# A grouped softmax: five tiles for six, one multiply a row, attached waits, loops not aligned

## Chip, cores and metric

The kernel runs on one core of one Trainium2 chip. The metric is the device time of one execution in microseconds (us); before the change it was 1332.67 us, the median of three runs (1332.51 to 1333.12). A run on the chip also leaves a profile; its one-page summary is called the page below, and its records of single instructions and transfers the trace. All profiled runs fell in the fast state, clock 1.000.

## The reference

An fp32 array of 16384 rows of 4352 numbers; each row is cut into eight groups of 544, and each group goes through a softmax.

```python
x_g = x.reshape(B, N, 8, 544)            # B, N = 4, 4096
x_g = x_g - x_g.max(axis=-1, keepdims=True)
exp = np.exp(x_g)
out = exp / exp.sum(axis=-1, keepdims=True)
```

285 MB come in and 285 MB go out.

## The kernel before

A tile is 256 rows of the array: 128 partitions with two rows each, 4352 KB. There are 64 tiles. The tiles live in a ring of six buffers. Three engines run their own programs. SyncE, called the queue's program below, issues the loads and stores. VectorE takes a row's eight maxima, later the reciprocals of the sums, and multiplies. ScalarE makes the exponentials and sums.

```python
def take(engine, sem, n=1):                    # a wait as an instruction of its own
    engine.sem_inc(sem, -n).wait_op(sem, n, "sem-ge")

def vector_scale(s):
    take(nc.vector, exp_done)
    nc.vector.reciprocal(out=rs[:, s, :], in_=sm[:, s, :]).then_inc(rec_done, 1)
    take(nc.vector, rec_done)
    xr = row(s)
    for g in range(G):
        i = nc.vector.tensor_scalar_mul(
            out=xr[:, g, :], in0=xr[:, g, :], scalar1=rs[:, s, g:g + 1])
    i.then_inc(scaled, 1)

def step(t, source, target):                   # the queue's program
    store(t, target)                           # waits until tile t is scaled
    take(nc.sync, stored[(t - 1) % NT], 16)    # the tile before has left
    load(t + AHEAD, source)                    # AHEAD = NT - 1
# ... cut ...
nc.sync.sem_inc(stored[NT - 1], 16)
for t in range(AHEAD):
    load(t, xt[t])
with nc.Fori(0, ring_turns, engines=OrderedEngineSet([nc.sync.engine]),
             head_slot={nc.sync.engine: 0}) as u:
    for t in range(NT):
        step(t, turn_in[u, t], turn_out[u, t])
# ... cut ...
with nc.Fori(0, turns, engines=OrderedEngineSet([nc.scalar.engine]),
             head_slot={nc.scalar.engine: 54}):
    for s in range(S):
        scalar_exp(s)
# ... cut ...
vector_max(0)
with nc.vector.Fori(0, turns):
    for s in range(S):
        vector_max((s + 1) % S)
        vector_scale(s)
```

With `head_slot` a loop asks for a place (slot) of its first instruction in a block of program: slot 0 for the queue's loop, slot 54 for ScalarE's. Such a loop is called aligned below.

## Time and profile before

| | before |
|---|---|
| time, median | 1332.67 us |
| span of the profiled run | 1331.4 us |
| transfers busy, of 16 DMA engines | 99.4% |
| VectorE / ScalarE busy | 78% / 57% |
| step of the queue (one load, one store) | 20.65 us |

A span runs from the first to the last instruction. The kernel is bound by its transfers, and the other engines wait for them; the prediction shows the lines.

### The profile page before, as it was taken

The numbers are of one execution on the slowest core, as the hardware profiler recorded it, in microseconds if no ns is written. First come the engines' busy times: TensorE is split into PE (matmuls) and PEld (weight loads), VectorE is DVE, ScalarE is ACT, GpSimd is POOL, SyncE is SP. The second block draws the span as 40 slices with busy tenths as digits, with TensorE's granted clock in tenths as the row PEclk, the third lists the DMA queues.
The fourth block names the chain that finished last, engine by engine and source line by source line (L and its number), as shares of the span: only waits on it lengthen the run. The fifth ranks groups of instructions, "written<-read, shape, count | busy, mean of one in ns | idle before, by whom it ended". The sixth has DMA issues, their size and how long they took to land. (4 is left out here: it accounts for less than half of the span.)

```text
span 1331.4 us, 4367 instructions
## 1 busy us (share of the span) xinstructions
DVE 1041.6 (78%) x1280; ACT 764.4 (57%) x2049; POOL 0.2 (0%) x4
## 2 busy tenths in 40 slices
DVE  4999987787877878778778787787877878778771
ACT  3777765655656556555565565655655556555560
POOL 0000000000000000000000000000000000000000
DMA  9999999999999999999999999999999999999997
GB/s 400 419 434 433 433 433 433 433 428 431 432 434 433 435 434 435 433 430 430 433 433 434 433 435 435 435 430 430 432 432 435 434 432 435 435 434 430 430 431 308
DMA packets 18441, 570.51 MB, mean 429 GB/s; under 512 B 2048, under 2 KB 2048, under 8 KB 2048
## 3 DMA queue, kind: packets, MB, share of 16 engines
q1 hardware_dynamic: 18432, 570.43, 99.4%
q14 instruction: 9, 0.07, 0.0%
HBM read 285.21 MB, written 285.21 MB: 428 GB/s over the span
## 5 line engine op out<-in xcount | busy, mean ns | idle before, releaser
L81 ACT ACTIVATE xt<-xt,mx 128x544 f32<-128x544 f32 x1024 | 751.2, 734 | 532.3 <-ACTq L56 532.3
L65 DVE TENSOR_REDUCE mx<-xt 128x8 f32<-128x4352 f32 x128 | 599.1, 4681 | 236.5 <-DVEq L56 236.4
L73 DVE TENSOR_SCALAR xt<-xt,rs 128x544 f32<-128x544 f32 x1024 | 434.1, 498 | 19.2 <-DVEq L56 0.2
L81 ACT ACTIVATION_READ_ACCUMULATOR xt<-xt,mx 128x1 f32 x1024 | 191.0, 187 | 0.0
L69 DVE RECIPROCAL rs<-sm 128x8 f32<-128x8 f32 x128 | 24.6, 192 | 4.2 <-DVEq L56 4.2
L120 ACT ACT_TABLE_LOAD x1 | 1.3, 1283 | 0.9 <-SPq L49 0.9
L153 POOL MEMSET const-bfloat16-1.0<- 128x1 bf16 x1 | 0.1, 103 | 0.0
L153 POOL MEMSET const-uint8-127<- 128x1 uint8 x1 | 0.1, 102 | 0.0
L153 POOL MEMSET const-float32-1.0<- 128x1 f32 x1 | 0.1, 100 | 0.0
L153 POOL MEMSET const-float32-0.0<- 128x1 f32 x1 | 0.1, 99 | 0.2 <-issue 0.2
## 6 DMA issues: line engine op xcount, KB each, us to landing
xt<-in_x_dram SPq DMA_DIRECT2D x64, 4352.0 KB, 30.7
out_dram<-xt SPq DMA_DIRECT2D x64, 4352.0 KB, 40.5
```

What stands on the lines that cost most here:

```text
L65: nc.vector.reduce_max(out=mx[:, s, :], in_=row(s), axis=X, negate=True).then_inc(max_done, 1)
L69: nc.vector.reciprocal(out=rs[:, s, :], in_=sm[:, s, :]).then_inc(rec_done, 1)
L73: i = nc.vector.tensor_scalar_mul(out=xr[:, g, :], in0=xr[:, g, :], scalar1=rs[:, s, g:g + 1])
L81: i = nc.scalar.activation(out=xr[:, g, :], in_=xr[:, g, :], func=Exp, bias=mx[:, s, g:g + 1], scale=1.0, accum_out=sm[:, s, g:g + 1],)
L120: nc.scalar.preload_act_table(Exp)
L153: nc = _bacc.Bacc("TRN2", target_bir_lowering=False, num_devices=1)
```

## The change

Its intent is a plainer kernel: less memory for the ring, fewer instructions, and no aligned loops.

```diff
-    NT = 6
+    NT = 5
 ...
     def vector_scale(s):
-        take(nc.vector, exp_done)
-        nc.vector.reciprocal(out=rs[:, s, :], in_=sm[:, s, :]).then_inc(rec_done, 1)
-        take(nc.vector, rec_done)
+        nc.vector.reciprocal(out=rs[:, s, :], in_=sm[:, s, :]).wait_op(
+            exp_done, s + 1, "sem-ge").then_inc(rec_done, 1)
         xr = row(s)
-        for g in range(G):
-            i = nc.vector.tensor_scalar_mul(
-                out=xr[:, g, :], in0=xr[:, g, :], scalar1=rs[:, s, g:g + 1])
-        i.then_inc(scaled, 1)
+        nc.vector.tensor_tensor(
+            out=xr,
+            in0=xr,
+            in1=rs[:, s, :].unsqueeze(2).to_broadcast([P, G, Dg]),
+            op=mybir.AluOpType.mult,
+        ).wait_op(rec_done, s + 1, "sem-ge").then_inc(scaled, 1)
 ... (the maximum and the exponential get attached waits in the same way)
-    with nc.Fori(
-            0, ring_turns, engines=OrderedEngineSet([nc.sync.engine]),
-            head_slot={nc.sync.engine: 0}) as u:
+    with nc.sync.Fori(0, ring_turns) as u:
 ...
-    with nc.Fori(
-            0, turns, engines=OrderedEngineSet([nc.scalar.engine]),
-            head_slot={nc.scalar.engine: 54}):
+    with nc.scalar.Fori(0, turns):
         for s in range(S):
             scalar_exp(s)
+        nc.scalar.sem_inc(max_done, -S)
 ...
+        nc.vector.sem_inc(exp_done, -S)        # at the end of VectorE's turn
+        nc.vector.sem_inc(rec_done, -S)
```

## The prediction

Passages that no trace or run of this case shows are cut out of the text, each cut marked. The sum: 1332.7 plus 0 to 2 us (start) and 0 to 1 us (end), put at 1333.3. The multiply's 4.69 us is an estimate from the maximum of the same row, which took 4.68 us (4.69 in the last line of the third view), and the 2% for the first rival rests on that estimate alone. The microseconds allowed at the turns and the 3 us for a changed mix of loads and stores are guesses; no trace showed them.

> **What bounds the kernel now.** I read the page first (busy shares, then the slices), then the queue's own issues in the timeline, then VectorE's timeline in the steady middle, at the start and at the end.
>
> ```profile
> DVE 1041.6 (78%) x1280; ACT 764.4 (57%) x2049; POOL 0.2 (0%) x4
> DMA  9999999999999999999999999999999999999997
> ...
> q1 hardware_dynamic: 18432, 570.43, 99.4%
> ...
> L81 ACT ACTIVATE xt<-xt,mx 128x544 f32<-128x544 f32 x1024 | 751.2, 734 | 532.3 <-ACTq L56 532.3
> L65 DVE TENSOR_REDUCE mx<-xt 128x8 f32<-128x4352 f32 x128 | 599.1, 4681 | 236.5 <-DVEq L56 236.4
> L73 DVE TENSOR_SCALAR xt<-xt,rs 128x544 f32<-128x544 f32 x1024 | 434.1, 498 | 19.2 <-DVEq L56 0.2
> ...
> xt<-in_x_dram SPq DMA_DIRECT2D x64, 4352.0 KB, 30.7
> out_dram<-xt SPq DMA_DIRECT2D x64, 4352.0 KB, 40.5
> ```
>
> The DMA engines are busy 99.4% of the span; VectorE is busy 78% and ScalarE 57%. VectorE's idle time stands almost wholly before the maximum (236.4 us), which waits for landings. So the transfers are the bound.
>
> ```profile
> 607.77 0.34 SPq L93 DMA_DIRECT2D xt<-in_x_dram  x1
> 608.36 0.35 SPq L97 DMA_DIRECT2D out_dram<-xt  x1
> 628.43 0.34 SPq L93 DMA_DIRECT2D xt<-in_x_dram  x1
> 628.95 0.35 SPq L97 DMA_DIRECT2D out_dram<-xt  x1
> ```
>
> One load and one store go out every 20.66 us, so a tile costs the queue 20.66 us and a transfer 10.33 us (2 x 4.456 MB in 20.66 us is 431 GB/s). 128 transfers of 10.33 us are 1322 us; the other 9 us of the span are the start and the last landing. A load takes 30.7 us to land, a store 40.5 us: with 10.33 us each, these are places three and four in a queue. On average (30.7 + 40.5)/20.66 = 3.4 transfers are under way.
>
> ```profile
> 597.32 4.68 DVE L65 TENSOR_REDUCE mx<-xt 128x8 f32<-128x4352 f32 x1 [4.04 <-DVEq L56]
> 601.92 0.19 DVE L69 RECIPROCAL rs<-sm 128x8 f32<-128x8 f32 x1
> 602.27 3.39 DVE L73 TENSOR_SCALAR xt<-xt,rs 128x544 f32<-128x544 f32 x8
> 605.58 4.68 DVE L65 TENSOR_REDUCE mx<-xt 128x8 f32<-128x4352 f32 x1
> 610.17 0.19 DVE L69 RECIPROCAL rs<-sm 128x8 f32<-128x8 f32 x1
> 610.51 3.39 DVE L73 TENSOR_SCALAR xt<-xt,rs 128x544 f32<-128x544 f32 x8
> 617.98 4.69 DVE L65 TENSOR_REDUCE mx<-xt 128x8 f32<-128x4352 f32 x1 [4.08 <-DVEq L56]
> ```
>
> This is one tile on VectorE: two rows of 8.26 us (597.32 to 605.58), then 4.08 us of waiting for the next landing. That 4.08 us is its whole room. The chain of waits to the end is cut off at the last multiply, which ends at 1301.5, 30 us before the span does: the rest is stores draining.
>
> [...] The loop ends of this trace cause no visible wait on VectorE, whose loop is not aligned before either; I allow a few microseconds a turn for the other engines.
>
> **The change, part by part.**
>
> (a) One multiply a row. Eight scalar multiplies of 3.39 us together become one two-tensor multiply of 4.69 us (estimate from [...] the reduction's 4.68). A row on VectorE becomes 8.26 + 1.30 = 9.56 us, a tile 19.1 us against 20.66 for its transfers. Busy time becomes 599.1 + 24.6 + 128 x 4.69 = 1224 us, 92%. Its room shrinks from 4.1 to 1.5 us a tile but stays above zero: cost to the end in the steady part, 0.
>
> (b) Waits attached to instructions. Before, each wait is its own semaphore instruction: 320 on VectorE of 21 ns (6.7 us in all), 128 on ScalarE of 17 ns. They go, and a few count-downs once a turn come. The busy chain of a row overlaps or hides most of them. Gain on the path: 0, since VectorE isn't the bound.
>
> (c) Five tiles for six. Time around the ring before: 6 x 20.66 = 124.0 us = 30.7 (load) + 29.0 (landing at 597.32 to the end of the tile's second multiply, 20.66 + 4.68 + 0.19 + 0.15 + 3.39) + 40.5 (store) + what is left, 23.8 us, in which a finished tile waits for its store to be issued because the queue's program stands at an earlier store's completion. With five: 5 x 20.66 = 103.3 = 30.7 + (29.0 + 1.3) + 40.5 + 1.8. The idle wait falls from 23.8 to 1.8 us, with the DMA queue just as deep. So the sixth tile was slack. Even if compute ran later, the first thing to shrink would be the queue of 3.4 transfers: more than two of them (about 25 us of work) can go before the engines run dry.
>
> (d) The start. Four loads are put out rather than five, so the queue is full up to about 15.95 + 3 x 10.33 = 46.9 us (the first maximum starts at 15.95, when load 0 has landed). The first store went out at 39.13; two longer multiplies come before it, so 41.7. That is 5 us ahead of the end of the loads. The first load needed 14.9 us from issue to landing, 4.5 us over its 10.33, part of it before the first byte, so the margin is 1 to 5 us. Load 4 follows at once. Later stores come every 19.1 us, slower than before but faster than 20.66, so the lead grows. Cost: 0 to 2 us.
>
> (e) The end. When the last tile lands (1278.58 before), four stores of 10.33 us remain instead of five, and the last must be there after three of them, 31.0 us later. Its compute before: 1278.58 to 1301.49, 22.9 us, with the multiplies of three rows in it: the one of the tile before, its first row's (beside which the exponentials run) and its last. Adding 1.3 us for each at most: 26.8 us. That is 4 us early, again less some of the start-up time. Cost: 0 to 1 us.
>
> (f) Loops not aligned. Twelve turns. VectorE can win back 1.5 us a tile, 7.7 us a turn, and ScalarE, which had 532 us of idle time, much more. The queue's program has two to three transfers ahead of it. Up to a few microseconds a turn are hidden.
>
> Sum: 1332.7 + 0 (steady) + 0 to 2 (start) + 0 to 1 (end) - 0, so 1333.3.
>
> **The rivals.**
>
> First: VectorE becomes the bound. It does if the multiply takes over about 5.5 us for a row (4.69 + 1.5/2 = 5.4). For it: 92% busy, with a broadcast operand not in the trace before. [...] If the multiply took 5.8 us, a tile would take 21.4 us, and 64 of them with start and end 1370 + 25 = about 1395 us. [...] I give this 2%.
>
> Second: the ring is too short. The 1.8 us in (c) could turn negative through jitter in landings or a stall at a loop's end. Then stores go out later and loads, which wait for stores, too. If the engines ran dry for 2 us at each of 12 turns, 1357 us. Against it: what shrinks first is the depth of the queue, not its busy time. I give a visible loss, over 5 us, 5%, most of it still within 2%.
>
> Third: the change is faster, because fewer semaphore and multiply instructions let VectorE hand over stores sooner. Against it: stores already wait 23.8 us before, so nothing earlier than that helps[...]. Under 1%. A shallower or differently mixed queue could change the rate by a few tenths of a per cent either way; that is most of my range.
>
> **Range and chances.** The steady rate varies between 428 and 435 GB/s among the slices, but averages over turns repeat to 0.05% in the three runs. Start and end can cost up to 3 us, a changed mix of loads and stores some 3 us either way, a small loss at the turns 3 us more. So 1333.3, with 1330 to 1339. Faster by over 2% would need 1306 us, under the 1322 us that the transfers take: 1%. Slower by over 2% needs 1360 us, the first rival or a bad case of the second: 3%.
>
> **What would show it right or wrong.** Right: DMA stays at 99% with the same GB/s; the multiply's group has 128 instructions of about 4.69 us; VectorE is about 92% busy; its wait before the maximum falls from 236 to about 236 - 128 x 1.3 = 70 us; ScalarE's busy time is unchanged; store issues come 0.5 us after load issues or up to some microseconds later, still every 20.66 us. Wrong: slices in which DMA falls below 9 or GB/s under 425, which names the stage (first two slices: start; last two: end; all over: ring or VectorE); a multiply of over 5.5 us; VectorE without any wait for landings in the steady part. [...]

## More of the kernel before

The page's part on DMA queues has one line for the data and this one for the program itself, with packets, MB and the share of sixteen engines' time:

```profile
q14 instruction: 9, 0.07, 0.0%
```

Nine packets of program, and a share that rounds to nothing.

## The result, and the profile after

The changed kernel took 1329.93 us, the median of four runs (1328.73 to 1330.95), against 1332.79 us for four runs of the kernel before. The ratio is 0.9978 with a 95% interval of 0.9961 to 0.9995. A ratio here is the mean time of one kernel's fast runs over that of the other's of the same rounds, so it is not quite the ratio of the medians quoted. The time lies 0.07 us below the predicted range of 1330 to 1339, and the prediction's sum had only terms that cost something, while the change gained 2.9 us. A miss of 0.07 us is far inside the spread of the four runs, so landing inside the range would have been luck: the gain has no term in the sum. It is worth asking where it came from.

The page of the kernel after, in the same parts as the prediction showed of before (busy engines, DMA slices, queues, groups of instructions, issues):

```profile
DVE 1207.7 (91%) x384; ACT 764.4 (58%) x2049; POOL 0.2 (0%) x4
...
DMA  9999999999999999999999999999999999999998
...
q1 hardware_dynamic: 18432, 570.43, 99.7%
q14 instruction: 3, 0.02, 0.0%
...
L82 ACT ACTIVATE xt<-xt,mx 128x544 f32<-128x544 f32 x1024 | 751.3, 734 | 539.2 <-DVE mx L63 539.2
L63 DVE TENSOR_REDUCE mx<-xt 128x8 f32<-128x4352 f32 x128 | 599.1, 4681 | 94.8 <-DMA xt<-in_x_dram 94.8
L72 DVE TENSOR_TENSOR xt<-xt,rs 128x4352 f32<-128x4352 f32 x128 | 600.6, 4692 | 4.4
...
xt<-in_x_dram SPq DMA_DIRECT2D x64, 4352.0 KB, 30.6
out_dram<-xt SPq DMA_DIRECT2D x64, 4352.0 KB, 40.3
```

Nearly everything is as foretold. The multiply takes 4692 ns. VectorE is busy 91%, and its wait before the maximum has shrunk from 236.4 to 94.8 us. Loads and stores land after 30.6 and 40.3 us, so the queue of transfers is as deep as with six tiles. What was not foretold is the second queue line: three packets of program for nine.

The queue's timeline after, in the steady middle (start, duration, engine, line, what was issued):

```profile
616.14 0.34 SPq L96 DMA_DIRECT2D xt<-in_x_dram  x1
616.66 0.35 SPq L100 DMA_DIRECT2D out_dram<-xt  x1
636.71 0.34 SPq L96 DMA_DIRECT2D xt<-in_x_dram  x1
637.63 0.35 SPq L100 DMA_DIRECT2D out_dram<-xt  x1
```

A step is 20.57 us (616.14 to 636.71), where the prediction's lines of before have 20.66 us. And the first maximum, which waits for the first landing, begins earlier. VectorE's timeline at the start (in brackets, how long the engine stood idle and what ended it), before:

```profile
15.95 9.28 DVE L65 TENSOR_REDUCE mx<-xt 128x8 f32<-128x4352 f32 x2 [15.95 <-DVEq L56]
```

and after:

```profile
13.90 9.28 DVE L63 TENSOR_REDUCE mx<-xt 128x8 f32<-128x4352 f32 x2 [13.90 <-DMA xt<-in_x_dram]
```

So there are two gains: 2.05 us at the first landing, and a shorter step. These two profiled runs lie further apart (1333.15 and 1328.73 us, 4.4 apart) than the medians, so the sizes read from them overstate the gain of 2.9 us.

**One level deeper: the sixteen engines.** A transfer is cut into 128 packets of 34,816 bytes, eight for each of sixteen DMA engines. In the trace most packets take 1288 ns, in both kernels (from 400 to 900 us 5964 of 6221 before, 6007 of 6222 after). A landing raises its semaphore sixteen times (2048 counts for 128 transfers), read here as once for each engine, and the wait ends with the sixteenth. I read these times from the trace's records, and call "lag" the time from the middle engine's count (between the eighth and the ninth) to the last one's.

| | first landing | its lag | lag at landing 33 of 128 | lag at the last but one | step, 400 to 900 us | last landing |
|---|---|---|---|---|---|---|
| before | 15.82 | 2.10 | 5.70 | 9.47 | 20.645 | 1330.04 |
| after | 13.88 | 0.38 | 4.15 | 3.74 | 20.567 | 1325.48 |

All in us. 20.567 us is sixteen packets of 1.2854 us, which is a packet's 1.288 us less the 3 ns or so by which neighbours overlap in the trace: in the steady part after, the last engine loses nothing. Before, the last engine loses another 0.078 us with each tile, through to the end; this is called the drift below. The middle engine gains nothing from the change (1330.04 - 9.46 = 1320.6 us before, 1325.48 - 3.74 = 1321.7 after, with the lags of the very last landing). The whole gain is that the last engine lags less.

The packet records of the kernel before show four packets of program of 8 KB, at 1.9, 7.1, 7.6 and 13.3 us, while the first loads are under way; they took 0.31 to 0.41 us each, 1.3 us in all. At the first landing the last engine came 1.31 us after the second last. The kernel after has no such packet before 38.7 us. This suggests a theory: program packets share the DMA engines with the data, and one engine that has to carry them lands its share of every transfer late.

### The profile page after: what moved, and what is told of

The parts are those of the page before. It is cut to its first block, busy times and chain, and to the rows that moved or that the text cites. A ratio compares the mean times of both kernels' runs of the same rounds, so it can differ in the third digit from the quotient of the medians.

```text
span 1326.8 us, 3155 instructions
## 1 busy us (share of the span) xinstructions
DVE 1207.7 (91%) x384; ACT 764.4 (58%) x2049; POOL 0.2 (0%) x4
## 2 busy tenths in 40 slices
DMA packets 18435, 570.46 MB, mean 430 GB/s; under 512 B 2048, under 2 KB 2048, under 8 KB 2048
## 3 DMA queue, kind: packets, MB, share of 16 engines
q1 hardware_dynamic: 18432, 570.43, 99.7%
## 5 line engine op out<-in xcount | busy, mean ns | idle before, releaser
L63 DVE TENSOR_REDUCE mx<-xt 128x8 f32<-128x4352 f32 x128 | 599.1, 4681 | 94.8 <-DMA xt<-in_x_dram 94.8
L72 DVE TENSOR_TENSOR xt<-xt,rs 128x4352 f32<-128x4352 f32 x128 | 600.6, 4692 | 4.4
## 6 DMA issues: line engine op xcount, KB each, us to landing
xt<-in_x_dram SPq DMA_DIRECT2D x64, 4352.0 KB, 30.6
out_dram<-xt SPq DMA_DIRECT2D x64, 4352.0 KB, 40.3
```

The source lines that it names most:

```text
L63: i = nc.vector.reduce_max(out=mx[:, s, :], in_=row(s), axis=X, negate=True)
L72: nc.vector.tensor_tensor(out=xr, in0=xr, in1=rs[:, s, :].unsqueeze(2).to_broadcast([P, G, Dg]), op=mybir.AluOpType.mult,).wait_op(rec_don ...
```

## The experiments

The theories: A, program fetched beside the first loads makes the gain. B, the ring of five tiles does. The prediction's own view was that nothing gains. Fifteen kernels ran, all correct.

### Which part of the change

**Five tiles only.** `NT = 6` becomes `NT = 5` in the kernel before.

> The kernel before with five tiles instead of six, nothing else. Theory A (the gain is instruction fetch: fewer instruction packets beside the first loads, so that no DMA engine starts late): still eight multiplies a row, so the first landing stays at 15.5 to 16 us and the time within 0.1% of before, 1332 to 1334. Theory B (the gain is the ring: with five tiles the sixteen DMA engines are spread apart less by the end): 1329 to 1331, and the steady step 20.57 us instead of 20.65. My recorded prediction held the sixth tile to be slack: 0.

1333.23 us, ratio 1.0004 (0.9987 to 1.0020); step 20.645 us. The ring gains nothing and loses nothing: theory B falls. The first landing came at 15.19 us, a little before the expected 15.5.

**One multiply only.** The eight `tensor_scalar_mul` of the kernel before become one `tensor_tensor`, with everything else left.

> The kernel before with one two-tensor multiply a row, six tiles, aligned loops and separate waits kept. Theory A (instruction fetch): VectorE's program shrinks by seven instructions a row, so the first landing comes at 14 to 14.5 us and the time is 1329.5 to 1331.5. Theory B (the ring): 1332 to 1334. VectorE about 92% busy either way; if VectorE were close to being the bound, over 1335.

1332.86 us, ratio 1.0001 (0.9984 to 1.0018). VectorE's shorter program did not help: theory A in its first form, that the multiplies' instructions are what is fetched, falls too. The four packets were still there, at 1.9, 6.6, 8.0 and 13.7 us.

**Loops and waits only.** The changed kernel with `NT = 6` and the eight multiplies put back.

> The changed kernel with six tiles and eight multiplies a row put back: only attached waits, counts once a turn and unaligned loops are left of the change. Theory A in its second form (padding for aligned loops is what is fetched): first landing at 14 to 14.5 us, 1330 to 1331.5. If the eight multiplies are what is fetched: 1332 to 1334 and the landing stays near 15.8. Theory B: 1332 to 1334.

1329.42 us, ratio 0.9977 (0.9960 to 0.9994), first landing 13.87 us, step 20.567 us. This part alone makes the whole gain. What the packets hold, padding or other program, no trace shows.

**The changed kernel again**, on the same chip.

> The changed kernel itself, on the chip of the three runs beside it: 1328.5 to 1331 again. If on this chip it does not differ from the kernel before, the 0.2% is a matter of chip or moment, not of the change.

1329.53 us, ratio 0.9981 (0.9965 to 0.9998). The gain repeats.

**Alignment or waits?** First the kernel before with its two aligned loops left unaligned, waits as they were:

```diff
-            head_slot={nc.sync.engine: 0}) as u:
+            ) as u:
-            head_slot={nc.scalar.engine: 54}):
+            ):
```

> The kernel before with the two aligned loops left unaligned, and nothing else; waits stay separate. If the alignment is the cause [...]: first landing near 14 us, 1329 to 1330.5. If the attached waits and the counts once a turn are the cause: landing near 15.5, 1332 to 1333.5.

1329.77 us, ratio 0.9978 (0.9961 to 0.9994), step 20.568 us. VectorE's first maximum in this run:

```profile
14.21 9.28 DVE L65 TENSOR_REDUCE mx<-xt 128x8 f32<-128x4352 f32 x2 [14.21 <-DVEq L56]
```

Then the reverse: the changed kernel with the two `head_slot` options put on.

> The changed kernel with the two loops aligned again as before. Alignment as the cause: landing at 15 us or later, 1331.5 to 1333.5, four or more program packets in the first 15 us. Attached waits as the cause: 1328.5 to 1331, landing near 14.

1332.20 us, ratio to before 0.9996 (0.9980 to 1.0013); four packets in the first 15 us again, first landing 14.86 us, step 20.621 us. Both directions agree: the aligned loops are what cost 3 us, and attached waits and counts are worth nothing that these runs can see.

### Which of the two loops

**Only ScalarE's loop aligned:**

> The kernel before with only ScalarE's loop aligned; the DMA queue's own loop is not. Theory: each aligned loop head that lies in another block costs one block, two packets of 8 KB, beside the first loads. The two packets at about 7 and 13 us moved with the loads when these were held back, so they belong to the queue's own loop. Here only two remain, at about 2 to 8 us: landing 14.3 to 15.3 us, 1330 to 1332.5.

1330.40 us, ratio 0.9983 (0.9966 to 0.9999). Two packets, at 1.9 and 6.9 us; first landing 14.33 us; step 20.580 us.

**Only the queue's own loop aligned:**

> The kernel before with only the DMA queue's own loop aligned. Two program packets, at about 7 and 13 us: landing 14.5 to 15.5 us, 1330.5 to 1333. If both loops count alike, this and the ScalarE-only run each keep about half of the 3.3 us; if the drift through the whole run comes with any packet beside the first loads, each keeps most of it.

1332.92 us, ratio 1.0002 (0.9985 to 1.0018). Two packets, at 8.0 and 13.7 us; first landing 15.01 us. Its start and its steady step in the timelines of VectorE and of the queue:

```profile
15.14 9.28 DVE L65 TENSOR_REDUCE mx<-xt 128x8 f32<-128x4352 f32 x2 [15.14 <-DVEq L56]
...
608.01 0.34 SPq L93 DMA_DIRECT2D xt<-in_x_dram  x1
...
628.65 0.34 SPq L93 DMA_DIRECT2D xt<-in_x_dram  x1
```

The step is 20.64 us. The queue's loop alone gives the time of the kernel before; ScalarE's costs little. I had expected halves as one possibility; it is not so.

**The queue's loop at another slot of a block.** `head_slot` 100 for 0, both loops aligned.

> The kernel before, both loops aligned, but the queue's own loop to slot 100 of its block rather than slot 0, where it can stand in the block that is already held. If fetched blocks and not alignment as such are the cause: two packets fewer in the first 15 us and a time like the ScalarE-only run, 1330 to 1332.5. If alignment as such: 1332.5 to 1333.5. [...]

1330.77 us, ratio 0.9988 (0.9971 to 1.0004). The queue's two packets are gone (only those at 1.9 and 6.9 us are left) and the step is 20.567 us. The interval of the ratio reaches over 1, so the time alone does not decide; the packets and the step say that it is not alignment as such, but whether the loop's place brings these two packets. That the loop's head then lies in a block that has to be fetched is the author's reading; the two packets are called the fetch of the loop's block below. In this run the drift began all the same at about 950 us (lag 5.1 us at landing 97, 6.4 at landing 127), with no program packet near it: the drift is not tied to such a fetch alone. The single packets, below, say why.

### Is it the fetch, and how does it cost

**Much more program.** 8192 semaphore instructions in a straight line for GpSimd, which has nothing to do, in the changed kernel:

```diff
+    for _ in range(4096):
+        nc.gpsimd.sem_inc(idle, 1)
+        nc.gpsimd.sem_inc(idle, -1)
```

> The changed kernel with 8192 semaphore instructions on the otherwise idle GpSimd, straight-line, at the start: about half a megabyte of program to fetch, some 64 packets of 0.31 us. If a fetch delays one of the sixteen DMA engines and the load ends with its slowest engine: 64 x 0.31 = 19.8 us on one engine, less the 4 us by which engines are apart anyway, so 1337 to 1350. If fetches spread evenly over sixteen engines: about 1.2 us, 1330 to 1332. If fetches have no part in it: 1328.5 to 1331.

1398.72 us, ratio 1.0494 (1.0477 to 1.0512): more than I expected. The page's rate by fortieths of the span and its program queue:

```profile
GB/s 402 424 430 430 429 430 431 435 420 404 400 401 390 398 403 395 392 393 400 402 418 409 423 422 412 416 417 410 416 414 424 434 431 418 428 416 404 420 359 264
...
q14 instruction: 67, 0.55, 0.1%
```

67 packets that hold 0.1% of the engines' time make the kernel 5% slower. Up to 280 us the mechanism is plain in the landings: one packet for each transfer, each of 309 ns, and landings come every 10.84 to 10.93 us rather than 10.29, about 0.6 us for one packet. A data packet just after one was long too: 1509 ns at 91.9 us, next to a program packet at 91.55 us. By 280 us the last engine lags 15.8 us, and by then it stands 10.5 us behind the second last: the delay falls on one engine. From 300 us on the rate falls for all engines (394 GB/s from 400 to 500 us, where the median data packet still takes 1288 ns but the mean is 1396 and the longest 3107). The run is 69 us longer than the changed kernel (1329.53); the packets' own cost is some 67 x 0.6 = 40 us of it, and I put the rest down to this second loss. What lengthens the packets is not explained by these runs.

**A few packets.** The same with 512 such instructions.

> The changed kernel, loops not aligned, with 512 semaphore instructions on the idle GpSimd: four or five program packets, 8 KB each, in the first 45 us, some 0.55 us each on one DMA engine as in the run with 8192. If packets early in the run are enough to start the slow drift of one engine (0.04 us a transfer), 1331.5 to 1333.5 and steps of 20.64 us; if they cost only themselves, the engine stays about 2 us further behind: 1329.5 to 1331.5 and steps of 20.57 us.

1329.72 us, ratio 0.9980 (0.9964 to 0.9997). Five packets, at 10.6 to 40.9 us, and the last engine is 2.6 us behind the middle one at the fifth landing. But the step is 20.567 us and the time is that of the changed kernel: the lag, 5.4 us at landing 33, held and did not grow. So a few packets early in the run are not enough to start the drift.

**Loads held back.** In the kernel before, eight small loads in turn go ahead of the first large one.

> The kernel before with its first load held back by eight small loads in turn, some 16 us, so that its program is fetched before the large loads begin. The time is longer by the hold H. If the fetches beside the first loads are the whole cause: 1329.5 + H, the sixteen engines within 0.5 us of each other at the first large landing. If alignment acts in another way too (the drift of one engine through the whole run): 1331.5 + H to 1333 + H.

1347.78 us, first large load issued at 15.20 us rather than 1.05. 1347.78 - 14.15 = 1333.6: no gain. The attempt missed its aim, for two of the four packets moved along, to 22.2 and 27.9 us. It still taught something: these two belong to the queue's program (with its loop alone aligned, two came at 8.0 and 13.7 us), and they come once it has issued its five loads, 22 MB: issued from 1.05 to 3.48 us before, with the packets at 7.6 and 13.3, and from 15.20 to 17.75 us here. So its block of program is fetched behind its own loads.

### How does the queue's loop keep one engine behind

**The block ahead of the loads.** The kernel before without aligned loops, but with an `addr_align` ahead of the queue's code, meant to move it to a fresh block before it issues anything:

```diff
+    nc.sync.addr_align(256, offset=0, max_nops=0)
     nc.sync.sem_inc(stored[NT - 1], 16)
     for t in range(AHEAD):
```

> The kernel before without aligned loops, but with the queue's own code moved to a fresh block ahead of its first loads: the block is fetched when no load is queued. If the loss and the drift come of packets fetched beside the first loads: no drift after 350 us, 1329 to 1331 (plus up to 2 us for the fetch itself, which then delays the first load visibly). If they come of the place of the queue's loop in a block: 1332 to 1333.5, drift of 0.04 us a transfer as in the run with only that loop aligned.

1333.92 us, ratio 1.0011 (0.9994 to 1.0027). The time alone would have deceived. The queue's first issues, VectorE's first maximum and the steady step:

```profile
3.61 4.37 SPq L93 DMA_DIRECT2D xt<-in_x_dram  x5
...
18.65 9.28 DVE L65 TENSOR_REDUCE mx<-xt 128x8 f32<-128x4352 f32 x2 [18.65 <-DVEq L56]
...
609.95 0.34 SPq L93 DMA_DIRECT2D xt<-in_x_dram  x1
...
630.51 0.34 SPq L93 DMA_DIRECT2D xt<-in_x_dram  x1
```

The step is 20.56 us, as without alignment: the drift is gone. The lag is 0.24 us at the first landing and stands at 4.0 us through the middle. But the queue started late, with program packets at 1.9 and 4.4 us; that it waited for them is inferred. Its first load went out at 3.61 us (1.05 before), took 2.37 us to issue rather than 0.39, and landed 4.4 us later than in the run without aligned loops (18.52 against 14.08 us). From the first landing to the last the two are alike: 1311.9 and 1312.1 us, against 1314.2 in the kernel before.

**Two packets from elsewhere.** GpSimd gets 80 semaphore instructions and an `addr_align`, meant to make it jump to a fresh block some microseconds after the start; loops not aligned.

> The kernel before without aligned loops, and the idle GpSimd made to jump to a fresh block some 7 us after the start: two program packets near 8 and 14 us, as the queue's own aligned loop has. If packets at that time start the drift: first landing near 15, 1332 to 1333.5. If they cost only themselves: landing 14.5 to 15.2, 1329.5 to 1331.5, no drift.

1329.37 us, ratio 0.9975 (0.9958 to 0.9992), step 20.567 us. Two program packets came, at 10.7 and 16.3 us, a little later than those of the queue (8.0 and 13.7). The lag at the second landing was 1.19 us, much like the 1.31 us of the run with only the queue's loop aligned. No drift followed until about 1000 us, and the time is that of the kernel without them. (From there on landings came every 10.32 us rather than 10.28, and the lag rose from 2.5 us at landing 97 to 4.5 at the end: the drift again, late.) So two packets beside the first loads cost nothing that the time shows if GpSimd causes them.

**A version to beat both.** The changed kernel, with stores issued by ScalarE on a queue of their own, after the first row of the next tile:

```diff
-        take(nc.sync, scaled, R)
-        nc.sync.dma_start(out=target, in_=bufs[t % NT][:, :]).then_inc(stored[t % NT], 16)
+        take(nc.scalar, scaled, R)
+        nc.scalar.dma_start(out=target, in_=bufs[t % NT][:, :]).then_inc(stored[t % NT], 16)
```

> A version meant to beat both: the changed kernel with the stores issued by ScalarE, after the first row of the next tile, on a queue of their own, so that a DMA engine need not turn from loads to stores in bursts. If the 4 to 5 us by which the slowest engine ends behind the median come of these turns: 1325 to 1329. If packets of two queues in turn cost more: slower, up to 1340.

1327.91 us (1327.47 to 1328.41), ratio to before 0.9966 (0.9949 to 0.9982). The page's queues:

```profile
q1 hardware_dynamic: 9216, 285.22, 49.9%
q10 hardware_dynamic: 9216, 285.22, 49.8%
q14 instruction: 4, 0.03, 0.0%
```

It beats the kernel before, and its median lies 1.6 us under that of the changed kernel's second set of runs (1329.53), but those are of other rounds and their ranges nearly touch (1328.55 is the lowest there), so against the changed kernel this is likely rather than shown. The lag at landing 33 is 1.1 us for 4.2, as hoped, but grows to 4.9 us before the last few landings. Its step, 20.62 us, is as long as with the drift, so it is not the steady part that gains. The edit also moves the stores to another moment, so this run does not tell which of the two, queue or moment, helps, nor whether turns from loads to stores cost a DMA engine anything: that was the guess.

### The runs side by side

Profiled run of each; lags, landing and step as defined above, "early" are program packets from 0 to 30 us.

| run | early packets at | first landing | last landing less first | step | time |
|---|---|---|---|---|---|
| before | 1.9, 7.1, 7.6, 13.3 | 15.82 | 1314.2 | 20.645 | 1332.67 |
| queue's loop aligned only | 8.0, 13.7 | 15.01 | 1315.3 | 20.644 | 1332.92 |
| after, loops aligned | 2.1, 6.8, 7.8, 13.5 | 14.86 | 1313.4 | 20.621 | 1332.20 |
| ScalarE's loop aligned only | 1.9, 6.9 | 14.33 | 1313.3 | 20.580 | 1330.40 |
| queue's loop at slot 100 | 1.9, 6.9 | 14.32 | 1312.9 | 20.567 | 1330.77 |
| block ahead of the loads | 1.9, 4.4 | 18.52 | 1311.9 | 20.567 | 1333.92 |
| two packets by GpSimd | 10.7, 16.3 | 14.22 | 1312.2 | 20.567 | 1329.37 |
| before, no loop aligned | none | 14.08 | 1312.1 | 20.568 | 1329.77 |
| after | none | 13.88 | 1311.6 | 20.567 | 1329.93 |

In all six runs in which the queue fetched its loop's block behind its own first loads (the three such rows here, and those with five tiles only, one multiply only and loads held back) the step stayed at 20.62 to 20.65 us. In none of the other runs with one queue for all transfers, but for that with 8192 instructions more, was it over 20.58 between 400 and 900 us.

**The single packets.** The trace does not name the engine of a packet, but most packets start 3 or 4 ns before another ends, read here as the one ahead of it on the same engine (in the trace before, the data packet at 7.371 us starts 4 ns before the program packet of 7.066 us ends), so each engine's packets can mostly be followed from one to the next. (Where two engines end within 2 ns of each other they can be mixed up.) Done for all runs, this answers part of the question:

- The loss is there in every kernel, the changed one too. Between 400 and 900 us, of some 6220 data packets 192 to 251 take 1289 to 1318 ns rather than 1288 (206 in the changed kernel, 220 before; the run with 8192 instructions is left out). With one queue they lie, as far as they can be followed, nearly all on one engine: 205 of the 206 in the changed kernel, 184 of the 220 before with most others lost from sight. They cost that engine about 0.06 us with each tile after and 0.08 before.
- What differs is whether this engine is the last one. In the kernel before it is: it carried both packets of the queue's program (7.55 and 13.33 us), ScalarE's at 7.07 us fell to another engine, and at no landing is it less than 0.30 us behind the second last. In the changed kernel it runs ahead of the last engine, by 4.5 us at 350 us and 1.9 us near the end, so its loss never shows.
- In all six runs in which the queue fetched its block behind its loads, its two packets fell to the engine with the long packets. GpSimd's two fell to another. In that run, and in the one with the loop at slot 100, the drift begins late, and the engine with the long packets is the last one by then.

Read so, the fetch does not start the drift. It sets a slightly slow engine behind all others, where its loss becomes the step. No run moved a fetch from one engine to another to test it.

## Why the prediction was wrong, point by point

**The bound: right.** Transfers held the time before and after (99.4% and 99.7% busy). But the prediction took the sixteen engines as one. The end is set by the slowest of them, which before lagged 9.5 us behind the middle one. That room for a gain stands on no line of the page; it takes the single engines' counts. (A slip beside it: "averages over turns repeat to 0.05%" rests on the times of three whole runs, 1332.51 to 1333.12 us; nothing shows turns.)

**(a) One multiply a row: right.** 4.69 us predicted, 4692 ns measured, and 91% busy for the 92% predicted. Alone it moved the time by a ratio of 1.0001. The wait before the maximum fell to 94.8 us rather than about 70. A row took less than the sum assumed: it runs from maximum to maximum in 9.43 us (29.46 to 38.89 in VectorE's timeline), not 9.56. Over 128 rows that is 17 of the 25 us; the rest is not accounted for.

**(b) Attached waits: right.** No gain seen; the kernel before without aligned loops, its waits still separate, has the time of the changed kernel.

**(c) Five tiles: right.** Ratio 1.0004 alone.

**(d) The start: wrong in sign.** The prediction said a cost of 0 to 2 us. The first store left at 39.24 us, ahead of the predicted 41.7, since the first landing came 2 us sooner. The prediction took the landing at 15.95 us as given, though a load of 10.3 us that needs 14.9 us should have been asked what the rest was. Of the 4.5 us over, 2 were the lag of one engine; 1.0 went by before the first packet started (issue at 1.05 us, packet at 2.08).

**(e) The end: right.** VectorE's end in the timeline after:

```profile
1284.39 4.68 DVE L63 TENSOR_REDUCE mx<-xt 128x8 f32<-128x4352 f32 x1 [1.66 <-DMA xt<-in_x_dram]
...
1304.78 4.69 DVE L72 TENSOR_TENSOR xt<-xt,rs 128x4352 f32<-128x4352 f32 x1
```

From the last landing to the last multiply's end it is 25.1 us (predicted 26.8 at most). The last landings follow one another in 10.3 us, so the last store was in time.

**(f) Loops not aligned: the step that failed.** It gave this part 0. The prediction looked for a cost of leaving them unaligned, stalls of engines at the turns "hidden" behind other work. It never asked what the aligned loops themselves cost. That was about 3 us: the kernel before without them ran in 0.9978 of its time, the changed kernel with them in 0.9996 of it. The cost was not where the prediction would have looked, in a waiting engine, but, as the packets are read above, in a DMA engine that carries the program and, set behind the others by it, ends every transfer. The sum thus lacked a term of about -3.3 us (1333.07 to 1329.77 us in the run without aligned loops); with it, and the start and the end at 0, it would have come to 1329.4.

**What stays open.** Shown: the gain is the unaligned loops; it is nearly all the queue's own loop; moving its fetch ahead of its loads takes the drift away. Also shown: a program packet delays one DMA engine by about 0.6 us, and a few such packets alone do not start the drift. Read from the packets of all runs, though no run was made for it: the drift is the loss of one engine that every kernel has, and it reaches the step where that engine is the last. Not settled: why that engine's packets are longer by 1 to 30 ns, why the queue's program fell to that engine in all six runs, and what makes the last engine of both kernels fall behind by 3.6 to 3.8 us up to landing 33.

## What to carry to other kernels

In these runs packets of program delayed the data (about 0.6 us of one DMA engine for each of the 309 ns packets in the run with 8192 instructions), and a transfer ended with its slowest engine, which in the kernel before came 9.5 us after the middle one. So when transfers fill the time, look at the single counts of a landing, not at the mean busy share, which was 99.4% and 99.7%. The queue's loop cost least unaligned (1329.77 us, no early packets) or at a slot that brought it no packets (1330.77 us, ScalarE's loop aligned too), and 2 to 3 us more with its two packets behind its own first loads (1332.92 us): where the engine that issues the transfers has an aligned loop, try the first two. Before calling a removed part harmless, ask what it cost while it was there.
